# A two-layer decoder trunk on one core: rest parts and sums around the gating unit's two seams moved to VectorE and widened

## The chip, the cores and the metric

The kernel runs on one core of a Trainium2 chip. The core has TensorE (PE in the profile, with its weight loads as PEld), VectorE (DVE), ScalarE (ACT), GpSimd (POOL) and SyncE (SP), whose queue issues most of the DMAs. Each engine works through its own instructions in order and waits on the others by semaphores. The metric is the device time of one execution in microseconds (us), as the median of three runs. All stage times below are counted from the start of the profiled span.

## The reference

The program computes two layers on 1024 tokens of width 1024. Layer 0 is latent attention, layer 1 a chunked gating unit; the change touches the gating unit alone.

```python
def sgu_branch(xn, w_in, ln_g, ln_b, w_s, b_s):
    u, v, gate = jnp.split(xn @ w_in, 3, axis=-1)          # three parts of 2048
    u = jax.nn.gelu(u, approximate=False)
    v = layer_norm(jax.nn.gelu(v, approximate=False), ln_g, ln_b)
    vb = v.reshape(B, S // CHUNK, CHUNK, SGU_GROUPS, SGU_GW)   # chunks of 128, 16 groups of 128
    w = jnp.where(tri[None], w_s, 0).astype(v.dtype)           # lower triangle
    sv = jnp.einsum('gts,bcsgd->bctgd', w, vb) + b_s.T[None, None, :, :, None]
    return u * sv.reshape(B, S, BRANCH_W) * jax.nn.silu(gate)

# layer 1 of the trunk, then the end
x = x + sgu_branch(rms_norm(x, norm_g[1]), ...) @ sgu_w_o
return rms_norm(x, final_g)
```

## The kernel before

**Numbers in two parts.** Each fp32 operand of a product is split into a high part (rounded to the matmul's format, written by ScalarE, line 100) and a rest part (the operand less its high part, line 101, on VectorE or GpSimd). A product is then three matmuls: high by high, high by rest, rest by high. In the rows `wh` and `wl` are the two parts of a weight tile, and `x` on line 101 or 816 is a tile that holds both parts of an activation.

**The projection (`sgu`).** The product with `w_in` is cut into 12 groups: u0, gate0, u1, gate1, four of v, u2, gate2, u3, gate3. Each group is a 2 x 2 block product done with seven products instead of eight (steps 1, 5, 6, 7, 2, 4, 3). The weight sums of a step are made on VectorE (lines 775 to 788); `prep` then splits the tile. The activation has four quarters in each block: `b11`, `b21` are the two halves of the channels for the first 512 tokens, `b12`, `b22` those for the last 512 (a "half" below is 512 tokens). Its seven sums or differences are made in place, once, by `sums(i)`, and split into `X[i]`; all groups use them. The order of steps is a list, `steps`: (0, 1), (1, 1), (0, 2), (1, 2), then 5, 6, 7, 4, 3, each for group 0 and group 1, then group after group. The weight tiles of a step are prepared two steps ahead (`ahead`), in four buffers that go round.

**The first seam.** Layer 0 ends with eight out-projection tiles `po` (added to `x` on line 548), and layer 1 starts with steps 1 and 2 of groups 0 and 1, which need only the first half of the tokens. The half's RMS scale is made as sum of squares (line 155), `rstd` (line 148 on VectorE, the power on GpSimd, line 149) and `spread` (lines 176 to 187: diagonal matrices, two matmuls into a bank `rb`). `normed` (line 917) applies it. The second half's squares are summed on line 904, its scale follows after step (0, 2), and is spread between the two halves of step (1, 2). Only then can `sums(5)` start.

**The second seam.** During the last group, `second_stage` starts the mixing of channel pair p = 0: `shift` and eight calls of `unit`, each with matmuls into a bank `sv` (there are two such banks at that time), two VectorE instructions that read it (lines 1096 and 1099, tile `ht`), and at the end of each half the product with u times gate (line 1102) and the split of the result (lines 100 and 101). `load_out(p)` loads and splits two tiles of the output weights. Then come, for p = 0 to 6, the out-projection items of p merged with the mixing of p + 1. `norm(p)` scales and splits v (line 1061 on ScalarE) once its DMA is in.

The order of the instructions on each engine comes out of a scheduler that works on the program as it is written. The list therefore moves in places that the diff doesn't name.

Of the kernel before, what the change touches and what calls it, by code (L numbers as in the profile page):

```python
# [66 lines left out]
class Builder:  # L67
# [658 lines left out]
    def sgu(self):  # L726
# [5 lines left out]
        with ExitStack() as st:  # L732
# [16 lines left out]
            with ExitStack() as s2:  # L749
# [18 lines left out]
                def prep(g, i):  # L768
                    R = lambda n: RAW[g, n]
                    if i == 1:  # L770
                        z = R("a0")
                    elif i == 5:
                        z = R("b1") if g < 2 else rp.tile([P, 1024], F32, tag="raw", name=self.nm("sum"))
                        RAW[g, "s"] = z
                        v.tensor_tensor(z, R("b0"), R("b1"), op=ALU.add)
                    elif i == 6:
                        z = R("s")
                        v.tensor_tensor(z, z, R("a0"), op=ALU.subtract)
                    elif i == 7:
                        z = R("b0")  # L780
                        v.tensor_tensor(z, R("a0"), z, op=ALU.subtract)
                    elif i == 2:
                        z = R("a1")
                    elif i == 4:
                        z = R("b1")
                    else:
                        z = R("s")
                        v.tensor_tensor(z, R("a1"), z, op=ALU.subtract)
                    wh, wl = (self.wp.tile([P, 1024], F32R, tag=t, name=self.nm(t)) for t in ("wh", "wl"))
                    self.split(wh, wl, z, nc.gpsimd if i in (1, 2, 4) else v)  # L790
                    return wh, wl


# [158 lines left out]


                def sums(i):
                    for k in range(4):
                        b11, b21, b12, b22 = (q_(kh, t, k) for t in range(2) for kh in range(2))
                        if i == 5:
                            normed(1, k)
                            v.tensor_tensor(b11, b12, b11, op=ALU.subtract)
                            cut(5, k, b11)  # L960
                        elif i == 6:
                            normed(1, 4 + k)
                            v.tensor_tensor(b11, b22, b11, op=ALU.subtract)
                            cut(6, k, b11)
                        elif i == 7:
                            v.tensor_tensor(b12, b22, b12, op=ALU.subtract)
                            cut(7, k, b12)
                        elif i == 4:
                            v.tensor_tensor(b21, b21, b11, op=ALU.subtract)
                            cut(4, k, b21)  # L970
                        else:
                            cut(3, k, b22)

                for q, (g, i) in enumerate(steps):
                    if g == 0 and i in (5, 6, 4, 3):
# [10 lines left out]
                    if q == 0:  # L986
                        for z in range(2):
                            open_banks(z, 1, B)
                        for k in range(4):
                            for z in range(2):  # L990
                                for s in range(2):
                                    quarter_product(z, 1, W[z], B, s, 0, k)
                        ahead(3)
                        work = self.wp.tile([P, 1024], F32R, tag="wl", name=self.nm("work"))
                        work = [work[:, half(z)] for z in range(2)]
                    elif q > 1:
                        product(g, i, W[q], B, (lambda: share(1, work)) if q == 3 else None)
                    if q == 2:
                        b = ps.tile([P, HALF], F32, tag="x", name=self.nm("ssq"))[:, :4]
                        for f in later:  # L1000
                            f()
                        v.tensor_tensor(tot[1, 0], tot[1, 0], tot[1, 1], op=ALU.add)
                        self.token_sums(b, tot[1, 0])
                        self.rstd(r[:, 4:], b, 1.0 / D, EPS)
# [19 lines left out]
    def second_stage(self, rs, nmr, ln, operand, rp, ps, pse):  # L1024
# [41 lines left out]
        def mix(p):  # L1066
# [12 lines left out]
            def unit(h, j, e):  # L1079
# [19 lines left out]
                nc.vector.scalar_tensor_tensor(th, b[:, :, 0], gain, th, op0=ALU.mult, op1=ALU.add)  # L1099
                if e == 1:  # L1100
                    t = t.rearrange("p c t -> p (c t)")
                    nc.gpsimd.tensor_tensor(t, t, U[p, j][:, half(h)], op=ALU.mult)  # L1102
                    self.split(hh[:, half(h)], hl[:, half(h)], t, nc.gpsimd)
            return [(1, shift)] + [(2, lambda z=z: unit(*z)) for z in np.ndindex(2, 2, 2)]

        def load_out(p):
            out = []
            for j in range(2):
                f = rp.tile([P, D], F32, tag="raw", name=self.nm("wf"))
                nc.sync.dma_start(f, a["w_so"][2 * p + j])  # L1110
                h, l = (self.wp.tile([P, 1024], F32R, tag=z, name=self.nm(z)) for z in ("wh", "wl"))
                for c in range(2):
                    self.split(h[:, half(c)], l[:, half(c)], f[:, half(c)], nc.gpsimd)
                out.append((h, l))
            return out

# [229 lines left out]
```

## Time and profile before

| | us |
|---|---|
| three runs | 1703.13, 1704.98, 1706.16 |
| median | 1704.98 |
| the profiled execution, device time | 1708.3 |
| its span, first to last instruction | 1706.6 |
| TensorE busy | 1664.1 |
| VectorE busy | 1084.5 |
| ScalarE busy | 730.2 |
| GpSimd busy | 566.8 |

The profiled execution is 3.3 us longer than the median of the runs, and 1.7 us of its time lie outside its span. [...] The engines' busy times overlap, and that of TensorE is made of matmuls that follow each other every 0.227 us (512 columns at the upper level).

### The profile page before, as it was taken

How to read it: one execution, taken by the hardware profiler on the slowest of the kernel's cores; microseconds unless marked ns; L12 is line 12 of the kernel's file. 1: busy time of each engine (PE TensorE's matmuls, PEld its weight loads, DVE VectorE, ACT ScalarE, POOL GpSimd, SP SyncE). 2: the span in 40 equal slices, each digit the busy share in tenths (PEclk: the TensorE clock that was granted, in tenths of full speed). 3: DMA queues.
4: the chain of work that ended last, by engine and by line, in shares of the span. 5: the costliest groups of instructions: out<-in, count | busy, mean ns of one | idle time of the engine just before them, and what ended most of it. 6: DMA issues, size and time to landing. Idle time of an engine off the chain costs nothing. (4 is left out here: it accounts for less than half of the span.)

```text
span 1706.6 us, 23986 instructions
## 1 busy us (share of the span) xinstructions
PE 1664.1 (98%) x9150; PEld 1440.3 (84%) x9150; DVE 1084.5 (64%) x2008; ACT 730.2 (43%) x1301; POOL 566.8 (33%) x423
## 2 busy tenths in 40 slices
PE   8999999999999999999999988999999999899996
PEld 7888888888888888888888767889999888788886
DVE  7452111777777777777777699545555444688977
ACT  6233222644444444444444556433333335544225
POOL 5355561211212121121211323232112252676663
PEclk9999999999999999999999999999999999899998
DMA  5054542211111110111110423223232143634302
GB/s 191 13 156 150 159 161 86 62 33 32 53 32 53 32 53 32 53 33 52 35 54 19 136 93 106 74 93 112 101 114 102 50 156 129 223 116 149 105 26 99
DMA packets 66884, 150.50 MB, mean 88 GB/s; under 512 B 9296, under 2 KB 19024, under 8 KB 65744
## 3 DMA queue, kind: packets, MB, share of 16 engines
q1 hardware_dynamic: 57152, 125.89, 22.8%
q10 hardware_dynamic: 9616, 23.07, 3.6%
q8 instruction: 72, 1.18, 0.3%
q14 instruction: 44, 0.36, 0.1%
HBM read 106.07 MB, written 38.15 MB: 85 GB/s over the span
## 5 line engine op out<-in xcount | busy, mean ns | idle before, releaser
L101 POOL TENSOR_TENSOR wl<-wf,wh 128x512 fp32r<-128x512 f32 (+1 forms) x156 | 196.3, 1276 | 402.7 <-ACT wh L100 402.2
L101 POOL TENSOR_TENSOR wl<-raw,wh 128x1024 fp32r<-128x1024 f32 x36 | 87.9, 2443 | 246.9 <-ACT wh L100 217.9
L606 ACT ACTIVATE p<-s,mx 128x128 f32<-128x128 f32 (+7 forms) x128 | 95.0, 742 | 124.2 <-DVE mx L604 122.3
L100 ACT ACTIVATE th<-pt 128x512 fp32r<-128x512 f32 (+1 forms) x160 | 88.4, 552 | 139.3 <-PE pt L630 138.5
L100 ACT ACTIVATE wh<-wf 128x512 fp32r<-128x512 f32 (+2 forms) x158 | 87.2, 582 | 88.8 <-PE pj L122 50.4
L816 PE MATMUL px<-x,wh 128*128 128x512 f32 x384 | 118.7, 390 | 1.6 <-ACT x L100 1.5
L121 PE MATMUL pj<-xnh,wh 128*128 128x512 f32 x304 | 119.5, 393 | 0.0
L122 PE MATMUL pj<-xnl,wh 128*128 128x512 f32 x304 | 119.2, 392 | 0.0
L123 PE MATMUL pj<-xnh,wl 128*128 128x512 f32 x304 | 119.1, 392 | 0.0
L101 DVE TENSOR_TENSOR tl<-pt,th 128x512 fp32r<-128x512 f32 (+1 forms) x160 | 101.1, 632 | 27.1 <-ACT th L100 26.2
L121 PE MATMUL po<-x,wh 128*128 128x512 f32 (+1 forms) x288 | 109.9, 382 | 0.0
L548 DVE TENSOR_TENSOR xt<-xt,po 128x512 f32<-128x512 f32 x128 | 87.4, 683 | 32.4 <-PE po L123 31.8
L121 PE MATMUL po<-oh,wh 128*128 128x512 f32 x256 | 106.5, 416 | 0.0
L122 PE MATMUL po<-x,wh 128*128 128x512 f32 (+1 forms) x288 | 105.7, 367 | 0.6 <-POOL x L101 0.6
L123 PE MATMUL po<-x,wl 128*128 128x512 f32 (+1 forms) x288 | 106.1, 368 | 0.0
L123 PE MATMUL po<-oh,wl 128*128 128x512 f32 x256 | 101.4, 396 | 0.0
L122 PE MATMUL po<-ol,wh 128*128 128x512 f32 x256 | 100.9, 394 | 0.0
L603 DVE TENSOR_REDUCE mx<-s 128x1 f32<-128x128 f32 (+7 forms) x128 | 96.8, 757 | 3.0
L1127 DVE TENSOR_TENSOR xt<-xt,po 128x512 f32<-128x512 f32 (+1 forms) x144 | 86.3, 621 | 16.2 <-PE po L123 15.9
L421 DVE TENSOR_TENSOR gate<-pj,rb 128x512 f32<-128x512 f32 x32 | 22.0, 690 | 116.1 <-PE pj L123 115.5
L630 PE MATMUL pt<-ident,p 128*128 128x128 f32 x576 | 90.3, 273 | 0.5 <-DVE p L608 0.4
L816 PE MATMUL py<-x,wh 128*128 128x512 f32 x256 | 84.1, 408 | 6.4 <-DVE x L101 5.1
(273 smaller groups left out, 4848.7 us busy)
## 6 DMA issues: line engine op xcount, KB each, us to landing
raw<-w_u_dram SPq DMA_DIRECT2D x18, 512.0 KB, 3.6
raw<-w_sg_dram SPq DMA_DIRECT2D x18, 512.0 KB, 3.7
wf<-w_gate_dram SPq DMA_DIRECT2D x32, 256.0 KB, 3.3
gate<-gate ACTq DMA_DIRECT2D x16, 512.0 KB, 3.9
wf<-w_o_dram SPq DMA_DIRECT2D x32, 256.0 KB, 2.8
gate<-gate SPq DMA_DIRECT2D x32, 256.0 KB, 2.6
raw<-w_v_dram SPq DMA_DIRECT2D x16, 512.0 KB, 3.5
v<-xt ACTq DMA_DIRECT2D x32, 256.0 KB, 2.0
```

What stands on the lines that cost most here:

```text
L100: self.nc.scalar.activation(hi, src, AF.Copy)
L101: (eng or self.nc.vector).tensor_tensor(lo, src, hi.bitcast(F32), op=ALU.subtract)
L121: nc.tensor.matmul(out, lh, rh, start=first, stop=False)
L122: nc.tensor.matmul(out, lh, rl, start=False, stop=False)
L123: nc.tensor.matmul(out, ll, rh, start=False, stop=last)
L421: nc.vector.tensor_tensor(g[:, c], b, rb[:, c], op=ALU.mult)
L548: nc.vector.tensor_tensor(x, x, st[m], op=ALU.add)
L603: nc.vector.tensor_reduce(mx, b, axis=AX.X, op=ALU.max)
L606: nc.scalar.activation(pr, b, AF.Exp, bias=mx, scale=SCALE, accum_out=sm)
L630: nc.tensor.transpose(b[:, w:w + P], PR[n, 4 * h + i][:, k * P:(k + 1) * P], self.ident)
L816: nc.tensor.matmul(o, l_, m_, start=opens and n == k == e == 0, stop=closes and n == 2 and k == 3 and e == (kind == "v"), skip_group_check ...
L1127: nc.vector.tensor_tensor(x, x, b, op=ALU.add)
```

## The change

Five edits, all in the gating unit:

1. The rest parts of the weight tiles of steps 1, 2 and 4 of groups 0 and 1 (six instructions of 128 x 1024) are made on VectorE instead of GpSimd.
2. `sums` works on several quarters at once: step 6 on two at a time, steps 7, 4 and 3 on all four, step 5 still on one. The difference and both parts of the split are one instruction each for 1024 or 2048 columns instead of 512.
3. The sums of the second half's squares and its scale are written after step (0, 1) instead of (0, 2), the spread inside step (0, 2) instead of (1, 2).
4. In `unit`, for p = 0, the product with u times gate and its rest part are on VectorE (four of each).
5. In `load_out`, for p = 0, the four rest parts are on VectorE.

```diff
-                    self.split(wh, wl, z, nc.gpsimd if i in (1, 2, 4) else v)
+                    self.split(wh, wl, z, nc.gpsimd if i in (1, 2, 4) and g > 1 else v)
...
                 def sums(i):
-                    for k in range(4):
-                        b11, b21, b12, b22 = (q_(kh, t, k) for t in range(2) for kh in range(2))
-                        if i == 5:
-                            normed(1, k)
-                            v.tensor_tensor(b11, b12, b11, op=ALU.subtract)
-                            cut(5, k, b11)
...
+                    n = {5: 1, 6: 2}.get(i, 4)
+                    for k in range(0, 4, n):
+                        b11, b21, b12, b22 = (
+                            self.xt[:, 4 * kh + k:4 * kh + k + n, half(t)] for t in range(2) for kh in range(2)
+                        )
+                        if i in (5, 6):
+                            for z in range(n):
+                                normed(1, (4 if i == 6 else 0) + k + z)
+                        a, b, out = {5: (b12, b11, b11), 6: (b22, b11, b11), 7: (b22, b12, b12),
+                                     4: (b21, b11, b21), 3: (b22, None, b22)}[i]
+                        if b is not None:
+                            v.tensor_tensor(out, a, b, op=ALU.subtract)
+                        self.split(X[i][:, 0, k:k + n], X[i][:, 1, k:k + n], out)
...
-                        product(g, i, W[q], B, (lambda: share(1, work)) if q == 3 else None)
-                    if q == 2:
+                        product(g, i, W[q], B, (lambda: share(1, work)) if q == 2 else None)
+                    if q == 0:
...
                 if e == 1:
-                    nc.gpsimd.tensor_tensor(t, t, U[p, j][:, half(h)], op=ALU.mult)
-                    self.split(hh[:, half(h)], hl[:, half(h)], t, nc.gpsimd)
+                    e = nc.gpsimd if p else nc.vector
+                    e.tensor_tensor(t, t, U[p, j][:, half(h)], op=ALU.mult)
+                    self.split(hh[:, half(h)], hl[:, half(h)], t, e)
...
-                    self.split(h[:, half(c)], l[:, half(c)], f[:, half(c)], nc.gpsimd)
+                    self.split(h[:, half(c)], l[:, half(c)], f[:, half(c)], nc.gpsimd if p else nc.vector)
```

What that does to VectorE's order at three places. The first is the start of the first seam, from the first half's sum of squares (`ssq`) to the first sums of step 1. Before:

```order
L735 CAST ones_r<-ones 128x128
L148 TENSOR_SCALAR small<-ssq_9966 128x4
L548 TENSOR_TENSOR xt<-xt,po_9989 128x512
L176 CAST rsh_9975<-small 128x4
L177 TENSOR_TENSOR rsl_9976<-small,rsh_9975 128x4
L186 TENSOR_SCALAR work_9973<-ident,rsh_9975 128x128 x4
L548 TENSOR_TENSOR xt<-xt,po_9999 128x512
L904 TENSOR_TENSOR x_2000_9915<-x_2000_9915 128x512
L548 TENSOR_TENSOR xt<-xt,po_10009 128x512
L917 SCALAR_TENSOR_TENSOR xt<-xt,ng,rb_9944 128x512 x3
```

And now:

```order
L735 CAST ones_r<-ones 128x128
L101 TENSOR_TENSOR wl_9929<-raw_9916,wh_9928 128x1024
L148 TENSOR_SCALAR small<-ssq_9966 128x4
L548 TENSOR_TENSOR xt<-xt,po_9989 128x512
L176 CAST rsh_9975<-small 128x4
L548 TENSOR_TENSOR xt<-xt,po_9999 128x512
L177 TENSOR_TENSOR rsl_9976<-small,rsh_9975 128x4
L186 TENSOR_SCALAR work_9973<-ident,rsh_9975 128x128 x4
L548 TENSOR_TENSOR xt<-xt,po_10009 128x512
L101 TENSOR_TENSOR wl_9933<-raw_9920,wh_9932 128x1024
L917 SCALAR_TENSOR_TENSOR xt<-xt,ng,rb_9944 128x512 x3
```

One weight rest part stands ahead of line 148, a second ahead of the first line 917; GpSimd has only the power of line 149 left here.

The second place is steps 6 and 7 of the activation, from the last scaling with `rb` on. `x_1996` is X[6], `x_1997` X[7]. Before:

```order
L917 SCALAR_TENSOR_TENSOR xt<-xt,ng,rb_9945 128x512 x2
L101 TENSOR_TENSOR x_1996_9911<-xt,x_1996_9911 128x512 x2
L963 TENSOR_TENSOR xt<-xt 128x512 x2
L101 TENSOR_TENSOR wl_10374<-raw_9924,wh_10373 128x1024
L101 TENSOR_TENSOR x_1996_9911<-xt,x_1996_9911 128x512 x2
L966 TENSOR_TENSOR xt<-xt 128x512 x2
L863 TENSOR_TENSOR cx<-px_10344,cx 128x512
L101 TENSOR_TENSOR x_1997_9912<-xt,x_1997_9912 128x512
```

And now:

```order
L917 SCALAR_TENSOR_TENSOR xt<-xt,ng,rb_9945 128x512 x2
L101 TENSOR_TENSOR x_1996_9911<-xt,x_1996_9911 128x1024
L966 TENSOR_TENSOR xt<-xt 128x2x512
L101 TENSOR_TENSOR wl_10368<-raw_9924,wh_10367 128x1024
L966 TENSOR_TENSOR xt<-xt 128x4x512
L101 TENSOR_TENSOR x_1996_9911<-xt,x_1996_9911 128x1024
L966 TENSOR_TENSOR xt<-xt 128x4x512
L863 TENSOR_TENSOR cx<-px_10338,cx 128x512
L863 TENSOR_TENSOR cx<-px_10339,cx 128x512
L101 TENSOR_TENSOR x_1997_9912<-xt,x_1997_9912 128x2048
```

The differences of steps 7 and 4 (128x4x512) now stand around the second rest part of step 6, and the rest part of step 7 comes as a whole after both reads of `px` (line 863).

The third place is the mixing of pair p = 0 in the second seam, around the banks `sv`; `x_2342` and `x_2320` with 128x1024 are splits of v for later pairs. Before:

```order
L1099 SCALAR_TENSOR_TENSOR ht_13819<-sv_13844,lngb,ht_13819 128x256
L871 TENSOR_TENSOR cx<-px_13689,cx 128x512
L101 TENSOR_TENSOR x_2320_13673<-x_2315_13641,x_2320_13673 128x1024
L871 TENSOR_TENSOR cx<-px_13690,cx 128x512
L1096 SCALAR_TENSOR_TENSOR ht_13819<-sv_13888,lngb,bs 128x256
L101 TENSOR_TENSOR x_2342_13887<-x_2315_13641,x_2342_13887 128x1024
L1099 SCALAR_TENSOR_TENSOR ht_13819<-sv_13888,lngb,ht_13819 128x256
```

And now (lines 1091 and 1094 are the former 1096 and 1099, line 1098 the former 1102; `x_2335` is the rest part of `ht`):

```order
L1094 SCALAR_TENSOR_TENSOR ht_13789<-sv_13814,lngb,ht_13789 128x256
L871 TENSOR_TENSOR cx<-px_13660,cx 128x512
L1098 TENSOR_TENSOR ht_13789<-ht_13789,x_2325_13691 128x512
L1091 SCALAR_TENSOR_TENSOR ht_13789<-sv_13858,lngb,bs 128x256
L1091 SCALAR_TENSOR_TENSOR ht_13789<-sv_13865,lngb,bs 128x256
L1094 SCALAR_TENSOR_TENSOR ht_13789<-sv_13858,lngb,ht_13789 128x256
L101 TENSOR_TENSOR x_2335_13782<-ht_13789,x_2328_13735 128x512
L1094 SCALAR_TENSOR_TENSOR ht_13789<-sv_13865,lngb,ht_13789 128x256
```

Between the two reads of the fifth bank (`sv_13888` before, `sv_13858` now) there stood a split of v; there now stands the first read of the sixth bank. Both splits of `x_2342` come after the eighth bank, those of `x_2320` after the first additions of the out-projection.

## Rows read from the trace of the kernel before

**Rows 1.** By stretch: busy us (count) of PE, PEld, DVE, ACT, POOL; clock; DMA.
```profile
970.00:1080.00 110.00, 97.38 (x404) 76.96 (x404) 97.96 (x132) 63.65 (x90) 33.04 (x17) 0.95 0.36 119
1080.00:1465.00 385.00, 385.00 (x2341) 346.31 (x2339) 193.88 (x261) 149.56 (x202) 113.05 (x62) 1.00 0.31 108
1465.00:1485.00 20.00, 14.19 (x56) 11.63 (x56) 13.84 (x18) 9.91 (x17) 16.11 (x11) 0.74 0.58 184
1485.00:1650.00 165.00, 165.00 (x823) 138.39 (x823) 137.75 (x251) 60.39 (x105) 109.70 (x83) 1.00 0.33 120
```
**Rows 2.** Waits of TensorE, 970 to 1080: total us, times, longest.
```profile
PE py L816 <- DVE x L101: 5.1, 3, 2.3
PE pb L816 <- DVE xt L548: 2.3, 2, 1.7
PE rb L187 <- DVE work L186: 1.9, 1, 1.9
PE px L816 <- ACT x L100: 1.5, 1, 1.5
PE py L816 <- ACT x L100: 1.3, 1, 1.3
```
**Rows 3.** Waits of TensorE, 1465 to 1485.
```profile
PE sv L1093 <- DVE ht L1099: 5.8, 1, 5.8
```
**Rows 4.** TensorE by stretch: busy (matmuls), granted clock, DMA share, GB/s.
```profile
977.00:981.00 4.00, 4.00 (x11) 0.59 0.98 355
1015.00:1019.00 4.00, 3.80 (x10) 0.57 0.01 2
1067.00:1070.00 3.00, 3.00 (x8) 0.52 0.22 87
1470.00:1479.50 9.50, 6.41 (x19) 0.50 0.73 227
```
**Rows 5.** Groups by form, 970 to 1080: busy us, mean ns, idle before.
```profile
L101 DVE TENSOR_TENSOR x<-xt,x 128x512 fp32r<-128x512 f32 x28 | 25.3, 939 | 0.3 <-ACT x L100 0.3
...
L101 POOL TENSOR_TENSOR wl<-raw,wh 128x1024 fp32r<-128x1024 f32 x7 | 18.4, 2627 | 40.9 <-PE px L816 26.4 <-ACT wh L100 11.9 <-ACT x L100 2.5
...
L966 DVE TENSOR_TENSOR xt<-xt 128x512 f32<-128x512 f32 x4 | 2.6, 685 | 0.0
...
L101 DVE TENSOR_TENSOR wl<-sum,wh 128x1024 fp32r<-128x1024 f32 x2 | 2.4, 1224 | 0.7 <-issue 0.7
```
**Rows 6.** Timeline of GpSimd from 972: start, duration, instruction, idle before.
```profile
972.30 2.40 POOL L101 TENSOR_TENSOR wl<-raw,wh 128x1024 fp32r<-128x1024 f32 x1 [1.99 <-ACT wh L100]
...
984.34 5.22 POOL L101 TENSOR_TENSOR wl<-raw,wh 128x1024 fp32r<-128x1024 f32 x2 [4.02 <-ACT wh L100]
```
**Rows 7.** Timeline of VectorE in the first seam.
```profile
986.37 3.73 DVE L101 TENSOR_TENSOR x<-xt,x 128x512 fp32r<-128x512 f32 x2
...
1008.63 1.41 DVE L917 SCALAR_TENSOR_TENSOR xt<-xt,ng,rb 128x512 f32<-128x512 f32 x2 [1.21 <-PE rb L187]
...
1062.28 5.04 DVE L101 TENSOR_TENSOR x<-xt,x 128x512 fp32r<-128x512 f32 x3
```
**Rows 8.** Timeline of GpSimd in the second seam.
```profile
1465.98 2.25 POOL L1102 TENSOR_TENSOR ht<-ht,x 128x512 f32<-128x512 f32 x1
```
**Rows 9.** Timeline of ScalarE in the second seam and behind it.
```profile
1468.27 0.63 ACT L100 ACTIVATE x<-ht 128x512 fp32r<-128x512 f32 x1 [2.17 <-POOL ht L1102]
...
1494.30 1.59 ACT L1061 ACTIVATE x<-x,small 128x256 f32<-128x256 f32 x3 [6.84 <-DMA x<-v]
```
**Rows 10.** Timeline of VectorE in the second seam.
```profile
1470.39 2.15 DVE L101 TENSOR_TENSOR x<-x,x 128x1024 fp32r<-128x1024 f32 x1 [2.30 <-ACT x L100]
1472.47 0.47 DVE L1099 SCALAR_TENSOR_TENSOR ht<-sv,lngb,ht 128x256 f32<-128x256 f32 x1
```
**Rows 11.** Timeline of GpSimd where the out-projection of pair 1 starts.
```profile
1506.22 1.29 POOL L101 TENSOR_TENSOR x<-ht,x 128x512 fp32r<-128x512 f32 x1 [0.74 <-ACT x L100]
```
**Rows 12.** Timeline of TensorE at the same place.
```profile
1507.87 0.39 PE L122 MATMUL po<-x,wh 128*128 128x512 f32 x1
```

More of the change, by code (lines that the diff above doesn't have):

```diff
@@ L954, in sums @@
                 def sums(i):
-                    for k in range(4):
-                        b11, b21, b12, b22 = (q_(kh, t, k) for t in range(2) for kh in range(2))
-                        if i == 5:
-                            normed(1, k)
-                            v.tensor_tensor(b11, b12, b11, op=ALU.subtract)
-                            cut(5, k, b11)
[L961 to L972, printed above, removed]
+                    n = {5: 1, 6: 2}.get(i, 4)
[11 more added lines that the diff above has]
+                        self.split(X[i][:, 0, k:k + n], X[i][:, 1, k:k + n], out)
                 for q, (g, i) in enumerate(steps):
```

## The prediction

> **What bounds the kernel now.** I read the busy times by stretch first [rows 1]. TensorE has no idle time from 1080 to 1465 and from 1485 to 1650, at the upper clock: there only fewer matmuls would save time, and the change leaves their number as it is. It loses time at two seams. From 970 to 1080 it is busy 97.4 of 110 us at a mean clock of 0.95, and VectorE is busy 98.0 of the 110. From 1465 to 1485 it is busy 14.2 of 20 us at 0.74.
>
> The waits of TensorE say for whom. In the first seam they add up to 12.1 us, nearly all for VectorE, or for a ScalarE split that itself follows VectorE [rows 2]. In the second it is one wait of 5.8 us for the second read of an `sv` bank [rows 3].
>
> A wait costs more than its length. Behind the waits the granted clock falls to about 0.5 [rows 4]. At 0.227 us per matmul the 11 matmuls from 977 to 981 need 2.5 us and take 4.0: 1.5 lost. From 1015 the 10 matmuls take 3.8 instead of 2.3 us: again 1.5. From 1067 the 8 take 3.0 instead of 1.8: 1.2. In the second seam 6.4 busy us at half clock lose 3.2. So the first seam costs 12.1 + 4.2 = 16.3 us, the second 5.8 + 3.2 = 9.0. These 25 us are all there is to win.
>
> **First seam, the moved rest parts.** Six GpSimd splits of 2.63 us become VectorE splits of 1.22 [rows 5], 7.3 us more for an engine that is already 89% busy there. Two things pay for them. GpSimd's split at 972.30 takes 2.40 us and stands ahead of the power in the first scale [rows 6]. Now the scale waits only for a 1.22 us split on VectorE. I put the bank `rb` about 1 us earlier and, as its two matmuls also stand later in TensorE's order, the 1.9 us wait at 0.6; a wait of 0.6 needs no clock loss behind it. Worth 1.3 + 1.5 = 2.8.
>
> Second, a VectorE instruction whose two inputs lie in SBUF stands still while GpSimd runs one: two splits from 986.37 took 3.73 us, ending 0.5 us after GpSimd's pair (984.34 + 5.22 = 989.56) [rows 6, 7], where 2 x 0.685 would do. The 28 splits of 512 columns average 0.939 against 0.685 [rows 5], 7.1 us in all; about 5 of these I trace to the six moved splits. So VectorE's added work is 7.3 - 5 = 2.3 us, less about 1 for the wide forms. The 2.3 us that TensorE waited for line 548 become about 1.6: that line now follows the scaling by 4 us instead of 6, but TensorE arrives almost 3 us sooner. Worth 0.7, and 3.5 up to the end of step 1.
>
> Wide forms: 1224 - 685 = 539 ns for 512 further columns [rows 5], so 128x2048 is estimated at 2.3 us, on ScalarE at about 2.0. Back to back, two of 512 took 1.28 to 1.41 on VectorE's timeline against 1.22 for one of 1024, a gain of some 0.1 us each. [...]
>
> **First seam, the second scale.** Its chain starts after the seven additions of squares, which now stand in a row. I follow VectorE's new order with these durations: the first scaling with the second `rb` comes at about 1006.7 instead of 1008.63 [rows 7]. TensorE, 3.5 us ahead, still waits for it, longer than now (about 4 us, with the clock loss), and ends step 5 only 1.5 us ahead. Bounds: 0 if the four remaining GpSimd products of line 853 hold VectorE there for another 1.5 us, 3.5 if the scale keeps pace.
>
> Step 6: its rest parts are now ready two at a time, 1 to 3 us ahead of the matmuls that read them, so the 1.5 us wait [rows 2] goes: 3.0 ahead. Step 7: TensorE gets nothing until all 2048 columns are split, behind both reads of `px`. By my walk that is some 0.4 us late: 2.6 ahead. Bounds: 0 to 3 (ScalarE 2.0 + VectorE 2.3 against 0.63 + 0.69 for a quarter). Steps 4 and 3: three quarter splits took 5.04 us from 1062.28 [rows 7] between two GpSimd instructions, and TensorE waited 3.0 us (two of the three waits behind 5.1) and lost 1.2 at half clock. Now the whole rest part stands earlier, at about 1054 to 1056, before TensorE needs it at 1058. Both come back: 2.6 + 4.2 = 6.8. I take **6.5** for the seam, with 3 and 8.5 as its bounds.
>
> **Second seam.** The 5.8 us wait goes back in a line: the second read of `sv` stood behind a split of v (1470.39, 2.15 us) [rows 10]; that waited for ScalarE, which had waited 2.17 us for GpSimd's product (1465.98, 2.25 us) [rows 8, 9]. GpSimd came to it late because it had four weight splits, and the products of line 853 between them. Now GpSimd has neither weights nor `ht`. VectorE takes over twelve instructions of 0.69 us, 8.2 us, in a stretch where it idles a third of the time, and the split of v stands behind the eighth bank. What is late next is VectorE: its reads come up to 1 us after TensorE wants the bank, four times, so I leave 1 us of the 9.0. Worth 8.
>
> Not all of it arrives. The out-projection of pair 1 needs its own rest parts, and GpSimd ended the second of them at 1506.22 + 1.29 = 1507.5 [rows 11], 0.36 us before the matmul that reads it, at 1507.87 [rows 12]. That chain starts with ScalarE, which waited 6.84 us for a DMA of v, until 1494.30 [rows 9]. The DMA queue holds this load until an earlier v is split and x is fetched. By the new order it is issued about 3.5 us sooner, not 8, and behind it GpSimd's queue is as long as before. I put the rest part at 1501.5, 6 us sooner, so 2 of the 8 are given back as a new wait at pair 1. Worth **6**, with bounds 3.5 (a clock loss there as well, and the DMA no more than 5 us sooner) and 8. Later pairs have over 2 us in hand and run as now.
>
> Sum: 6.5 + 6 = 12.5. The profiled 1708.3 become 1695.8; its 3.3 us over the median taken off, **1692.5 us**.
>
> **Rivals.** (A) The first seam wins nothing: VectorE sets its pace, and 2.3 us more work with whole-row splits makes new waits at steps 5 and 7 (2 + 3 us and 1.5 of clock) in place of 6.5 us won. For it: 98 of 110 us busy. Against it: a tenth of those are waits for GpSimd that go. Then 1704.98 - 6 = 1699. (B) The second seam gives its 8 us back at pair 1 but for 1 us, since the DMA of v is bound by the volume of x, u, v and weights that goes through at once; 1704.98 - 7.5 = 1697.5. (C) The other sign: the hold itself. VectorE issues six wide and twelve short two-input instructions more, and the products left on GpSimd hold them. If all 7.1 us of holding stay in the first seam, the added 7.3 us fall on the path with one more clock loss of 1.5, 8.8 us lost; if eight products of 1.29 us in the second seam also hold VectorE, 10 us, its 9.0 are lost again and 1 more. Then 1704.98 + 9.8 = 1714.8. It decides once VectorE is held for more than some 6 us that are free now. Against it: far fewer GpSimd instructions remain. [...] (D) The waits only move, and both scale and v bind as now: within 0.2%, 1704.
>
> **How the numbers follow.** Forecast 0.64, A 0.12, B 0.10, C 0.06, D 0.08. The forecast's own range, from 9 to 16 us won, is 1689 to 1696. With A and B, and some width for a second clock loss, the range is **1686.5 to 1700.5**; it leaves out C and D and the edges. No change means within 0.2%, 3.4 us, about what three runs can tell: faster 0.86, the same 0.08, slower 0.06.
>
> **What would show it.** Line 101 on GpSimd from 970 to about 1070 once instead of seven times; 18 GpSimd instructions fewer in all. No wait of TensorE for line 548 over 1.7 us, none of 2 us at step 3, but one of 3 to 5 us at step 5. No half clock around 978 and 1068. In the second seam no wait over 1.5 us for the second `sv` read, and the first out-projection about 8 us nearer to the last projection step. At pair 1 a wait of about 2 us, for GpSimd. The step most likely wrong is the walk through step 5 and 7: an order says what follows what, not when, and a slip of 1 us decides whether the clock falls.

## The result and the profile after

Four runs of the changed kernel gave 1693.23 to 1696.28 us, median 1695.13; four of the kernel before, on the same chip, 1703.13 to 1706.16, median 1704.22. The ratio is 0.9935 with a 95% interval of 0.9922 to 0.9949, that is 11 us (9 to 13) faster; the two medians alone are 9.1 us apart. The predicted 12.5 us lie inside the interval, near its upper end. The forecast time of 1692.5 us is 2.6 us below the measured median, which lies inside the forecast's range. Measured once more on another chip (run 9 below) the ratio was 0.9928 (0.9909 to 0.9947). The sum came near; both seams' terms were off, in opposite directions.

The profiled execution took 1695.74 us (span 1693.9, mean clock 0.992). Its stretches, with the columns of [rows 1], the third one new:

```profile
970.00:1080.00 110.00, 102.97 (x444) 83.00 (x444) 98.92 (x120) 63.35 (x80) 24.16 (x13) 0.98 0.35 120
1465.00:1485.00 20.00, 20.00 (x103) 16.86 (x102) 15.75 (x29) 9.18 (x17) 5.73 (x6) 1.00 0.68 245
1485.00:1540.00 55.00, 51.36 (x239) 42.23 (x238) 45.47 (x79) 24.19 (x45) 40.06 (x30) 0.94 0.34 125
```

TensorE's idle time in the first stretch fell from 12.6 to 7.0 us, the second stretch is full, and a hole has opened in the third, where TensorE had none before. GpSimd did 17 instructions in the first stretch and does 13. The waits of TensorE from 970 to 1080, against [rows 2]:

```profile
PE py L816 <- ACT x L100: 4.2, 1, 4.2
PE pb L816 <- DVE xt L548: 1.3, 1, 1.3
PE rb L187 <- DVE work L186: 1.0, 1, 1.0
PE px L816 <- DVE x L101: 0.3, 1, 0.3
PE py L816 <- DVE x L101: 0.2, 1, 0.2
```

One long wait is left, the one at step 5. The groups by form, against [rows 5]:

```profile
L101 POOL TENSOR_TENSOR wl<-raw,wh 128x1024 fp32r<-128x1024 f32 x3 | 7.9, 2636 | 8.3 <-ACT c L852 4.2 <-ACT wh L100 4.1
L101 DVE TENSOR_TENSOR x<-xt,x 128x512 fp32r<-128x512 f32 x12 | 7.9, 684 | 0.0
...
L101 DVE TENSOR_TENSOR x<-xt,x 128x2048 fp32r<-128x2048 f32 x3 | 7.4, 2454 | 0.0
...
L966 DVE TENSOR_TENSOR xt<-xt 128x2048 f32<-128x2048 f32 x2 | 4.6, 2287 | 0.0
```

GpSimd has three weight splits instead of seven in this stretch (the first at 1054.62), and a VectorE split of 512 columns takes 0.684 us instead of 0.939: nothing holds it any more. The wide splits still average 2.454 us, where a difference of the same 2048 columns takes 2.287.

**A ledger.** The times at which TensorE starts the same matmul show where the time came from. The first matmul on the squares' sums stands ahead of everything that the change touches, and came at 970.37 before and 967.47 now: 2.9 us are not the change's. The other columns are "ahead of before" in us, worked out from such times, with each kernel's difference at that first mark taken off. A number that grows from one row to the next is time won in between, one that falls is time given back.

| TensorE starts | before | changed | ahead: changed | changed, again | first seam alone | second seam alone | pair 1's weights too |
|---|---|---|---|---|---|---|---|
| sums of squares | 970.37 | 967.47 | 0 | 0 | 0 | 0 | 0 |
| step 1 | 984.69 | 978.84 | 2.95 | 3.05 | 3.03 | 1.69 | 3.03 |
| step 5 | 1011.94 | 1007.93 | 1.11 | 1.24 | 1.17 | 2.04 | 1.17 |
| step 6 | 1028.59 | 1021.03 | 4.66 | 5.05 | 5.00 | 1.17 | 4.87 |
| step 3 | 1061.73 | 1054.32 | 4.51 | 4.92 | 4.90 | 1.13 | 4.76 |
| group 2 | 1077.66 | 1065.20 | 9.56 | 9.97 | 9.95 | 1.02 | 9.81 |
| first out-projection | 1480.97 | 1460.17 | 17.90 | 18.38 | 10.42 | 9.41 | 18.20 |
| weight sums of pair 2 | 1508.33 | 1492.34 | 13.09 | 14.14 | 9.47 | 7.23 | 18.21 |
| weight sums of pair 3 | 1534.46 | 1520.73 | 10.83 | 11.77 | 9.43 | 7.21 | 17.27 |
| last sums of squares | 1695.54 | 1682.79 | 9.85 | 10.88 | 8.64 | 6.50 | 17.29 |

The first seam won 9.56 us where 6.5 were predicted. The second won 17.90 - 9.56 = 8.3 (predicted 8), and by pair 3 17.90 - 10.83 = 7.1 of them were given back (predicted 2).

**Two columns that were not the change's.** The second-seam column is of a kernel whose first seam is as before, and it is "1.02 ahead" there; two more such kernels are 1.79 and 1.88 ahead. The clock tells why. TensorE from 40 to 60 and from 975 to 985, before and then in one of these kernels, that of run 10 (the granted clock is the third number from the end of a line; in stretches of 0.5 us of before it is 1.00, the upper level, or 0.50, half clock, or a figure between in a stretch in which it changes, and at 0.50 matmuls of 512 columns start 0.43 us apart):

```profile
40.00:60.00 20.00, 20.00 (x92) 17.07 (x91) 8.47 (x24) 5.19 (x13) 3.50 (x3) 0.83 0.09 16
975.00:985.00 10.00, 7.46 (x25) 5.69 (x26) 7.93 (x17) 7.04 (x12) 4.05 (x3) 0.83 0.82 283
```

```profile
40.00:60.00 20.00, 20.00 (x106) 17.13 (x105) 8.46 (x25) 5.78 (x14) 3.50 (x3) 1.00 0.08 15
975.00:985.00 10.00, 8.77 (x38) 6.66 (x36) 10.00 (x14) 6.29 (x10) 5.73 (x3) 1.00 0.76 281
```

The profiled execution of before fell to half clock (0.50 from 978.0 to 981.0) behind a 1.9 us wait; there run 10 waited 1.3 us and kept its clock. About 1.6 us (the mean of 1.02, 1.79 and 1.88) of the first seam's 9.56 belong to that one execution. What the change wins there is about 8.0. The length of the wait alone doesn't decide it: run 12 waited as long for the same matmul and kept the upper level.

```profile
973.90 0.50 PE L187 MATMUL rb<-work,ones_r 128*128 128x512 f32 x1 [1.93 <-DVE work L186]
```

```profile
975.00:985.00 10.00, 7.62 (x31) 5.16 (x30) 9.68 (x14) 6.21 (x11) 2.37 (x1) 1.00 0.54 207
```

The stretch from 40 to 60, far ahead of the change, shows 0.83, 0.91 or 1.00 in nine profiles (before, the changed kernel, which has 0.91 twice, and runs 1 to 3 and 10 to 12), and with it the first mark lies at 970 to 971, 967 to 969 or 966 to 967. The scatter between profiles has that as one source.

### The profile page after: what moved, and what is told of

The parts are those of the page before. It is cut to its first block, busy times and chain, and to the rows that moved or that the text cites. A ratio compares the mean times of both kernels' runs of the same rounds, so it can differ in the third digit from the quotient of the medians.

```text
span 1693.9 us, 23943 instructions
## 1 busy us (share of the span) xinstructions
PE 1659.1 (98%) x9150; PEld 1437.1 (85%) x9150; DVE 1094.9 (65%) x2007; ACT 728.6 (43%) x1290; POOL 531.9 (31%) x405
## 4 chain that ended last, share of the span: by engine, by line
PE 92%; DVE 3%; POOL 2%; ACT 2%; issue 1%; DMA 0%; POOLq 0%; SPq 0%; ACTq 0%; DVEq 0%
PE px L816 11%; PE py L816 8%; PE pb L816 8%; PE pj L121 7%; PE pj L122 7%; PE pj L123 7%; PE po L121 6%; PE po L123 6%; PE po L122 6%; PE pt L630 4%; PE pv L123 3%; PE pv L121 3%; PE pv L122 3%; PE s L121 2%; PE s L122 2%; PE s L594 2%
## 5 line engine op out<-in xcount | busy, mean ns | idle before, releaser
L101 POOL TENSOR_TENSOR wl<-wf,wh 128x512 fp32r<-128x512 f32 (+1 forms) x152 | 189.0, 1261 | 404.1 <-ACT wh L100 403.5
L101 POOL TENSOR_TENSOR wl<-raw,wh 128x1024 fp32r<-128x1024 f32 x30 | 72.7, 2424 | 209.7 <-ACT wh L100 202.5
L121 PE MATMUL po<-x,wh 128*128 128x512 f32 (+1 forms) x288 | 111.4, 387 | 2.3 <-ACT x L100 1.6
L122 PE MATMUL po<-x,wh 128*128 128x512 f32 (+1 forms) x288 | 107.6, 374 | 2.2 <-POOL x L101 2.2
L1123 DVE TENSOR_TENSOR xt<-xt,po 128x512 f32<-128x512 f32 (+1 forms) x144 | 86.6, 621 | 15.7 <-PE po L123 15.2
L100 ACT ACTIVATE wh<-raw 128x1024 fp32r<-128x1024 f32 x54 | 56.8, 1056 | 67.1 <-PE py L816 24.8
```

Source lines behind the costliest of these rows:

```text
L100: self.nc.scalar.activation(hi, src, AF.Copy)
L101: (eng or self.nc.vector).tensor_tensor(lo, src, hi.bitcast(F32), op=ALU.subtract)
L121: nc.tensor.matmul(out, lh, rh, start=first, stop=False)
L122: nc.tensor.matmul(out, lh, rl, start=False, stop=False)
L1123: nc.vector.tensor_tensor(x, x, b, op=ALU.add)
```

## The experiments

Twelve experiments, each against runs of the kernel before on the same chip. A gain in us is worked out from the ratio; the difference of the medians lies up to 2 us from it. "Ahead" is by the ledger.

**1. The first seam alone** (edits 1 to 3). The diff is against the changed kernel: it takes edits 4 and 5 back.

```diff
-                    e = nc.gpsimd if p else nc.vector
-                    e.tensor_tensor(t, t, U[p, j][:, half(h)], op=ALU.mult)
-                    self.split(hh[:, half(h)], hl[:, half(h)], t, e)
+                    nc.gpsimd.tensor_tensor(t, t, U[p, j][:, half(h)], op=ALU.mult)
+                    self.split(hh[:, half(h)], hl[:, half(h)], t, nc.gpsimd)
...
-                    self.split(h[:, half(c)], l[:, half(c)], f[:, half(c)], nc.gpsimd if p else nc.vector)
+                    self.split(h[:, half(c)], l[:, half(c)], f[:, half(c)], nc.gpsimd)
```

> Kernel before plus the three edits of the first seam (rest parts, wide sums, sooner scale); the second seam as before. Theory (the seams add up, and the first seam won about 9.6 us between the squares' sums and the seventh step's end in the profiles): 9 to 10 us faster than before, so about as fast as the whole change; TensorE's 5.8 us wait for the second sv bank is there again, and no wait at the start of the next pair's out-projection. Rival (the first seam gives the 6.5 us predicted, and the rest of its 9.6 us is spread between two executions): 6 to 7 us faster.

Ratio 0.9950 (0.9935 to 0.9965), 8.5 us faster (6 to 11). Ahead by 9.95 at group 2 and 8.64 at the end; the 5.9 us wait for `sv` is there. Together with the 1.6 us above this lies between the two expectations: about 8.4 won, part of the 9.6 from one execution.

**2. The second seam alone** (edits 4 and 5 on the kernel before).

```diff
-                    nc.gpsimd.tensor_tensor(t, t, U[p, j][:, half(h)], op=ALU.mult)
-                    self.split(hh[:, half(h)], hl[:, half(h)], t, nc.gpsimd)
+                    e = nc.gpsimd if p else nc.vector
+                    e.tensor_tensor(t, t, U[p, j][:, half(h)], op=ALU.mult)
+                    self.split(hh[:, half(h)], hl[:, half(h)], t, e)
...
-                    self.split(h[:, half(c)], l[:, half(c)], f[:, half(c)], nc.gpsimd)
+                    self.split(h[:, half(c)], l[:, half(c)], f[:, half(c)], nc.gpsimd if p else nc.vector)
```

> Kernel before plus the two edits of the second seam alone (product and rest parts of pair 0, and its four weight splits, on VectorE). Theory (won 8.3 us at the last projection step, 7.1 us given back one pair later): within 0.5 to 2 us of before, faster; the 5.8 us wait gone, waits of 3 to 4 us and half a clock when pair 1's out-projection starts. Rival (the give-back belongs to the two seams together): 5 to 6 us faster, as predicted for this seam.

Ratio 0.9965 (0.9953 to 0.9977), 6.0 us faster (4 to 8). The theory fell: alone, this seam keeps what the prediction gave it. It won 9.41 - 1.02 = 8.4 and gave back 2.2. The same instructions in the same order give back 2.2 here and 7.1 in the changed kernel. ScalarE here, and TensorE (two stretches of 4 us) where pair 1's out-projection starts:

```profile
1484.89 5.04 ACT L1061 ACTIVATE x<-x,small 128x256 f32<-128x256 f32 x10 [9.75 <-DMA x<-v]
1489.83 0.62 ACT L100 ACTIVATE x<-ht 128x512 fp32r<-128x512 f32 x1
```

```profile
1495.38:1499.38 4.00, 3.31 (x16) 2.25 (x15) 3.96 (x7) 1.52 (x3) 4.00 (x4) 1.00 0.00 0
1499.38:1503.38 4.00, 3.02 (x15) 2.60 (x16) 3.02 (x7) 3.37 (x7) 3.26 (x3) 1.00 0.19 47
```

And in the changed kernel: ScalarE, GpSimd, and TensorE in stretches of 4 us:

```profile
1474.80 4.05 ACT L1056 ACTIVATE x<-x,small 128x256 f32<-128x256 f32 x8 [10.82 <-DMA x<-v]
1479.88 1.09 ACT L1056 ACTIVATE x<-x,small 128x256 f32<-128x256 f32 x2 [1.03 <-DMA x<-v]
1480.87 0.61 ACT L100 ACTIVATE x<-ht 128x512 fp32r<-128x512 f32 x1
...
1488.84 0.63 ACT L100 ACTIVATE x<-ht 128x512 fp32r<-128x512 f32 x1 [3.83 <-POOL ht L1098]
```

```profile
1476.81 1.30 POOL L1098 TENSOR_TENSOR ht<-ht,x 128x512 f32<-128x512 f32 x1 [1.29 <-DVE ht L1094]
1481.57 1.30 POOL L101 TENSOR_TENSOR x<-ht,x 128x512 fp32r<-128x512 f32 x1 [3.45 <-ACT x L100]
1482.82 4.76 POOL L101 TENSOR_TENSOR wl<-wf,wh 128x512 fp32r<-128x512 f32 x3
1487.53 1.27 POOL L1098 TENSOR_TENSOR ht<-ht,x 128x512 f32<-128x512 f32 x1
1488.76 1.28 POOL L101 TENSOR_TENSOR wl<-wf,wh 128x512 fp32r<-128x512 f32 x1
1490.00 1.27 POOL L101 TENSOR_TENSOR x<-ht,x 128x512 fp32r<-128x512 f32 x1
```

```profile
1484.17:1488.17 4.00, 3.02 (x15) 2.13 (x14) 3.09 (x5) 0.84 (x1) 4.00 (x3) 1.00 0.00 0
1488.17:1492.17 4.00, 1.35 (x3) 0.94 (x4) 2.20 (x5) 3.09 (x6) 4.00 (x4) 0.77 0.00 0
1492.17:1496.17 4.00, 4.00 (x13) 3.23 (x12) 3.62 (x6) 1.89 (x3) 3.26 (x3) 0.50 0.48 164
1496.17:1500.17 4.00, 4.00 (x19) 3.31 (x19) 4.00 (x10) 0.63 (x1) 1.89 (x2) 0.87 0.59 205
```

ScalarE's order has ten scalings of v (eight of pair 3, two of pair 4) ahead of pair 1's first high part. Here pair 4's v was in when its turn came, and the ten stand in a row: the two loads landed 7.1 and 4.8 us after their issue. In the changed kernel, which issues them as far behind the first out-projection matmul as here (6.3 and 11.6 us), they took 8.3 and 8.1 us from their issue to the scaling that they let go (1466.51 to 1474.80, 1471.76 to 1479.88). ScalarE stopped twice, and the first high part came 20.70 us after the first out-projection matmul instead of 18.45. TensorE then lost 3.6 us to waits instead of 1.7, the clock fell to half behind them, and that cost the other 3.4 (7.1 - 3.6).

**3. The changed kernel with pair 1's four weight splits on VectorE too.**

```diff
-                    self.split(h[:, half(c)], l[:, half(c)], f[:, half(c)], nc.gpsimd if p else nc.vector)
+                    self.split(h[:, half(c)], l[:, half(c)], f[:, half(c)], nc.gpsimd if p > 1 else nc.vector)
```

> The changed kernel, with the four weight splits of pair 1 on VectorE as well. Theory Q (GpSimd's queue: the weight splits stand between the first and the second rest part of pair 1, 6 of the 9.7 us from 1481.57 to 1491.27): the waits of 1.6 and 1.3 us and the half clock behind them go, 4 to 6 us faster than the changed kernel, about 1690. Theory D (ScalarE is late because it stands waiting for the DMA of v, until 1474.80 and again until 1479.88, and everything behind it is late by as much): at most 1 us faster.

Median 1691.12, ratio 0.9911 (0.9896 to 0.9925), 15 us faster than before. As theory Q has it, nothing is given back at pair 1 (18.20, 18.21), and the end is 17.29 ahead, where the changed kernel was 9.85 and 10.88. GpSimd at the same place:

```profile
1481.94 1.29 POOL L101 TENSOR_TENSOR x<-ht,x 128x512 fp32r<-128x512 f32 x1 [1.48 <-ACT x L100]
1485.85 1.29 POOL L1098 TENSOR_TENSOR ht<-ht,x 128x512 f32<-128x512 f32 x1 [2.62 <-DVE ht L1094]
1487.88 1.29 POOL L101 TENSOR_TENSOR x<-ht,x 128x512 fp32r<-128x512 f32 x1 [0.74 <-ACT x L100]
```

GpSimd now idles 2.62 us ahead of the second product, which waits for VectorE. The v was early in this profile too (first high part 18.70 us after the first out-projection matmul), but by this slack a v that lands 2 us later should not have delayed that product, so that a late v would cost time only through the weight splits that queue behind the first rest part. That is argued: the three kernels without these splits on GpSimd (runs 3, 4 and 12) all have an early v in their profiles (first high part after 18.70, 18.49 and 17.97 us). What the queue costs behind an early v is 2.2 to 2.9 us (runs 2 and 8); how the rest of the changed kernel's 7 is shared between the queue and a late v, no profile separates.

**4. The same, with the norm of pair 2's v written behind pair 1's units.**

```diff
-                norm(p + 2, fetch(p + 2))
+                c = fetch(p + 2)
+                if p:
+                    norm(p + 2, c)
                 run(self.merge(items[head:], mix(p + 1)))
+                if p == 0:
+                    norm(p + 2, c)
```

> As the run with pair 1's weight splits on VectorE, and the norm of pair 2's v written behind pair 1's units instead of ahead of them, so that ScalarE comes to pair 1's high parts one activation sooner and TensorE to its sv banks one out-projection tile sooner. Theory Q: the same as without it within 1 us. Theory D: 1 to 3 us faster than without it.

Median 1690.03, ratio 0.9906 (0.9891 to 0.9922): the same within 1.1 us, as Q has it. ScalarE's order on the way to the first high part is one scaling shorter, no more, so this is a weak test of D. These two have the lowest medians of the study. Against the changed kernel their intervals touch its own; the ledger has run 3 ahead of it by 6.4 to 7.4 us.

**5. The moved rest parts alone** (edit 1).

```diff
-                    self.split(wh, wl, z, nc.gpsimd if i in (1, 2, 4) else v)
+                    self.split(wh, wl, z, nc.gpsimd if i in (1, 2, 4) and g > 1 else v)
```

> Kernel before plus the moved rest parts alone (six GpSimd splits of two groups to VectorE). By the prediction's walk: 3.5 us ahead up to the end of the second step, then part of it lost where the second scale is still late: 1 to 4 us faster than before. Rival (VectorE is the pace there, and 7.3 us more work costs more than the hold that goes): 1 to 4 us slower.

Ratio 1.0003 (0.9993 to 1.0012): no gain, and no loss. Both expectations missed. The splits of 512 columns fall to 0.835 us. But the 4.2 us wait at step 5 is there as in the changed kernel (0.77 ahead, where unchanged seams are about 2.0), and quarter splits are still waited for at step 3 (two waits, 2.6 us).

**6. The wide sums alone** (edit 2, the part of the change's diff on `sums`).

```diff
-                    for k in range(4):
...
+                    n = {5: 1, 6: 2}.get(i, 4)
+                    for k in range(0, 4, n):
...
+                        self.split(X[i][:, 0, k:k + n], X[i][:, 1, k:k + n], out)
```

> Kernel before plus the wide sums alone. By the prediction: they only save some 1 us of VectorE, and hide the waits of steps 6 to 3 by standing earlier as a whole: 1 to 5 us faster. Rival (a whole row must be split before TensorE gets anything): up to 3 us slower, with a new wait at the start of steps 6 or 7.

Ratio 0.9987 (0.9978 to 0.9996), 2.2 us faster, at the low end of the expected. Ahead 4.01 at group 2, 2.4 above the 1.6 of an unchanged seam.

**7. The sooner second scale alone** (edit 3).

```diff
-                        product(g, i, W[q], B, (lambda: share(1, work)) if q == 3 else None)
-                    if q == 2:
+                        product(g, i, W[q], B, (lambda: share(1, work)) if q == 2 else None)
+                    if q == 0:
```

> Kernel before plus the sooner second scale alone. By the prediction: the wait of step 5 shrinks by 1 to 2 us when VectorE is still held by GpSimd's splits: 0 to 3 us faster. Rival (the additions of squares now stand ahead of the scaling that TensorE waits for in the second step): up to 2 us slower.

Ratio 0.9977 (0.9966 to 0.9987), 3.9 us faster, a little over the expected. Step 6 starts 5.21 ahead, but TensorE then waits 3.1 us for ScalarE and 3.1 for VectorE in steps 6 to 4, and gets back only at step 3 (4.56 at group 2).

**8. The changed kernel without the wide sums.**

```diff
-                    n = {5: 1, 6: 2}.get(i, 4)
-                    for k in range(0, 4, n):
...
+                    for k in range(4):
...
```

> The changed kernel with the old quarter-wide sums (the other four edits kept). If the three edits of the first seam add up, slower than the changed kernel by what the wide sums alone win over before. Rival (with GpSimd's splits gone there is nothing to hold the short sums, so the wide form wins nothing more): within 1 us of the changed kernel.

Ratio 0.9957 (0.9942 to 0.9972), 7.3 us faster than before, some 4 less than the changed kernel. The rival fell, and the theory's sum was too small as well (the wide sums alone won 2.2). At group 2 it is 2.97 ahead instead of 9.56: the wide sums are worth 6.6 us there once the other two edits stand, and 2.4 by themselves. TensorE's waits are those that the prediction spoke of, quarter splits at step 3:

```profile
1059.34 0.50 PE L816 MATMUL py<-x,wh 128*128 128x512 f32 x1 [0.89 <-DVE x L101]
1062.11 0.72 PE L816 MATMUL py<-x,wh 128*128 128x512 f32 x1 [1.81 <-DVE x L101]
```

Pair 1 took back only 11.24 - 8.39 = 2.9 here; its first high part came 19.11 us after the first out-projection matmul.

**9. The changed kernel again**, with no edit.

> The changed kernel once more, with a profile of its own. In its first profile v landed 8.3 and 8.1 us after its issue, TensorE waited 3.6 us where pair 1's out-projection starts, ran at half clock behind it, and 7.1 us of the 8.3 won at the second seam were given back; the run with the second seam alone had v after 7.2 us, waits of 1.7 us, no half clock, and gave back 2.2. Theory J (the schedule is the same, and about 1 us in the landing of v decides whether the clock falls): the executions scatter by 4 us or more, the profile shows a give-back anywhere from 2 to 7 us that follows the landing of v, and the ratio is about 0.992 to 0.995. Theory F (with the first seam won too, the give-back is always 7): a give-back of 6 to 8 us whatever v does, and 9 us faster than before.

Ratio 0.9928 (0.9909 to 0.9947), six runs from 1690.43 to 1697.87. The first high part came 20.10 us after the first out-projection matmul, and 6.6 us were given back. With the numbers above that makes 18.45, 19.11, 20.10 and 20.70 us beside 2.2, 2.9, 6.6 and 7.1 us given back: theory J fits, with a step between 19.1 and 20.1. A first seam that is won doesn't by itself make v late: runs 3, 4 and 12 won it too, issue the first of the two loads at the same distance, and have their first high part after 17.97 to 18.70 us. J isn't settled against F, since both profiles of this very kernel lie above the step, and the kernel before scatters as widely (1700.72 to 1708.87).

**10. and 11. The second seam's two edits one at a time** on the kernel before: first the product and rest part (edit 4), then the weight splits (edit 5).

```diff
-                    nc.gpsimd.tensor_tensor(t, t, U[p, j][:, half(h)], op=ALU.mult)
-                    self.split(hh[:, half(h)], hl[:, half(h)], t, nc.gpsimd)
+                    e = nc.gpsimd if p else nc.vector
+                    e.tensor_tensor(t, t, U[p, j][:, half(h)], op=ALU.mult)
+                    self.split(hh[:, half(h)], hl[:, half(h)], t, e)
```

```diff
-                    self.split(h[:, half(c)], l[:, half(c)], f[:, half(c)], nc.gpsimd)
+                    self.split(h[:, half(c)], l[:, half(c)], f[:, half(c)], nc.gpsimd if p else nc.vector)
```

> Kernel before plus one edit of the second seam: product and rest part of pair 0 on VectorE, its four weight splits left on GpSimd. By the prediction, the wait came from GpSimd's product standing behind the weight splits: without the product the 5.8 us wait goes, 4 to 7 us faster than before. Rival (the weight splits themselves, then late, hold VectorE's new two-input instructions and the out-projection's start): 0 to 3 us faster, and a wait of 1 us or more at the first out-projection.

> Kernel before plus the other edit of the second seam: pair 0's four weight splits on VectorE, product and rest part left on GpSimd. GpSimd comes to its products about 5 us sooner, but each rest part still goes from VectorE to GpSimd to ScalarE to GpSimd. Theory (the queue on GpSimd made the wait): the 5.8 us wait shrinks to 0 to 2 us, 4 to 6 us faster. Rival (the chain from engine to engine made it): it stays at 4 us or more, 0 to 2 us faster.

The product alone: ratio 0.9973 (0.9962 to 0.9984), 4.6 us faster; 7.07 - 1.79 = 5.3 won at the first out-projection, a wait of 1.9 us for `sv` left, 1.6 given back. The weights alone: ratio 0.9995 (0.9983 to 1.0007), no change that shows. Yet they took the 5.8 us wait away but for 1.0 us (9.71 - 1.88 = 7.8 won at the first out-projection, so the queue on GpSimd made the wait), and by pair 3 9.71 - 1.56 = 8.2 us were given back: at pair 1 TensorE waited 1.7 us for ScalarE and 1.6 for a bank `sv`, and its clock fell to half (0.50 from 1504 to 1508). The theory was right on the wait, the rival on the time.

**12. The run of 3 with group 1's rest parts back on GpSimd.**

```diff
-                    self.split(wh, wl, z, nc.gpsimd if i in (1, 2, 4) and g > 1 else v)
+                    self.split(wh, wl, z, nc.gpsimd if i in (1, 2, 4) and g > 0 else v)
```

> The changed kernel with pair 1's weight splits on VectorE as well, and the rest parts of the second group of the first seam back on GpSimd (only the first group's moved). In the profile of the changed kernel VectorE has two splits of 1.2 and 1.5 us and a sum between the second rb and the sums that step 5 waits 4.2 us for, while GpSimd idles. Theory (VectorE's own work makes that wait): it shrinks to 2 to 3 us, 1 to 3 us faster than the run with pair 1's weight splits alone. Rival (each GpSimd split holds a pair of VectorE splits again): the same, or up to 3 us slower than that run.

Ratio 0.9929 (0.9910 to 0.9948), not faster than run 3. At step 5 the 4.2 us fell to 2.5, as the theory has it, but new waits stand elsewhere (970 to 1080), and the seam is 7.70 ahead instead of 9.81:

```profile
PE pb L816 <- DVE x L101: 2.4, 3, 1.9
PE px L816 <- ACT x L100: 1.9, 1, 1.9
PE rb L187 <- DVE work L186: 1.9, 1, 1.9
PE py L816 <- DVE x L101: 1.3, 1, 1.3
PE py L816 <- ACT x L100: 1.2, 1, 1.2
```

VectorE's splits of 512 columns are back at 0.822 us. TensorE kept the upper level through the whole stretch, so no clock loss is among them:

```profile
970.00:1080.00 110.00, 100.86 (x436) 79.90 (x435) 99.38 (x113) 62.66 (x80) 31.91 (x16) 1.00 0.33 117
```

The rival is the nearer one: the ledger's end is 15.2 ahead instead of 17.29, and the ratios lie some 3 us apart (0.9929 against 0.9911, on another chip, with intervals that overlap).

## Why the prediction was right, and where not

**First seam, the moved rest parts (predicted 3.5 up to the end of step 1).** Right in mechanism: 2.95 at the start of step 1, and behind it the second wait for line 548 (1.68 us) is gone, 4.6 in all. Kernels with this seam unchanged are 1.6 to 1.7 ahead at the same mark and wait 1.3 us behind it, so 2.1 of the 4.6 belong to before's execution and 2.5 to the change. Alone the edit wins nothing (run 5): the microseconds won here are waited away at steps 5 and 3 unless the other edits stand.

**The second scale (predicted 1.5 ahead at the end of step 5).** The wait of 3 to 5 us at step 5 came (4.2), with a half clock behind it (0.50 from 1009.5 to 1012.0). But TensorE was 4.66 ahead at the start of step 6, where 3.0 were predicted. Before, it had lost 3.3 us to two waits and 1.5 to the clock there; the second of these waits is gone (0.2). This term was too small by 1.7 us.

**Steps 6, 7, 4 and 3.** Step 7 cost 0.15 between the starts of steps 6 and 3 (predicted 0.4; a wait of 0.31 shows it). Step 3 brought 9.56 - 4.51 = 5.05 (predicted 4.2). Run 8 shows the reason as it was given: without the wide form the quarter splits wait there again. For the price of the wide form the durations are 0.680, 1.222 and 2.287 us for 512, 1024 and 2048 columns, so four of 512 one by one are 2.72. Back to back they cost less: six additions of 512 took 3.70 us, 0.617 each, so four are 2.47 against 2.29 for the wide one, as the sum had it. The prediction took about 1 us off for the wide forms, at some 0.1 an instruction; on VectorE 19 instructions go (28 splits became 17, and 16 differences 8), which at 0.1 each is nearer 2 us, and 1.1 at the 0.06 of these additions. Run 8 has the same seam lose 6.6 us without them: wide instructions won more by where they stand than by what they save.

**The seam's sum.** 6.5 was predicted with 3 and 8.5 as bounds; the profiles show 9.6 to 10.0, outside. The 3.1 us between 6.5 and 9.56 are the second scale (1.7), step 3 (0.9), step 7 (0.2) and the rounding of 6.8 to 6.5 (0.3). Another step failed beside these sizes: the 1.5 us of half clock around 978 were booked as the kernel's, and only the execution profiled before shows them. Without that execution's 1.6 us the seam won 8.0 to 8.4, inside the bounds, near the upper one.

**Second seam.** The 8 won were 8.3, and by the mechanism named: run 11 takes 4.8 of the 5.8 us of wait away by emptying GpSimd's queue, run 10 takes 3.9.

**Given back at pair 1 (predicted 2, bounds 0 and 4.5).** 7.1 and 6.6 in the two profiles of the changed kernel, 2.2 with the second seam alone. The place, ScalarE's stop for v and the queue on GpSimd were named; the size failed. By the prediction the second rest part would end 6 us sooner. Less the 12.46 us by which all of this stretch had moved (9.56 and the 2.9 of the first mark), its chain gained this: the load of v that ScalarE waits for was issued 15.14 - 12.46 = 2.7 us sooner (1486.90 to 1471.76; predicted 3.5), it landed 2.0 sooner, the first rest part started 2.5 sooner, and the second ended (1507.51 to 1491.27) 3.8 sooner. And no clock loss was in the 2; behind 3.6 us of waits it was 3.4. Rival B is what the profile shows (1.3 us of the second seam are left), but the volume of the loads, its reason, isn't what run 3 shows: with the same loads, and a v that was early, nothing is given back there.

**The rest.** GpSimd has 18 instructions fewer. Rivals A, C and D fell: the seam won, and VectorE's short splits were no longer held (0.684 us). That GpSimd can be held instead shows as well: three splits took 4.76 us beside a VectorE split at 1485.04, and 3.81 in run 2. VectorE's own hold shows before on the two splits from 986.37 [rows 7], and not on line 548 ahead of them, which reads TensorE's `po` and took 0.68 us at 985.77 beside the same pair on GpSimd. The hold on GpSimd doesn't explain what is given back: run 8 has it as well (4.83 us) and gave back 2.9, and in run 2 the product behind the three splits took 2.31 us instead of 1.27, so GpSimd lost 1 us there too.

The forecast held because two errors went against each other: the first seam gave 1.5 us more than its term (3 by the profiles as they are), the second 4 to 5 less. What is left is somewhat below 12.5: the ledger ends 9.85 and 10.88 ahead, 1.6 of it by before's execution, and the medians are 9.1 and 10.8 us apart. That the total came so near is in part luck.

## What to carry to other kernels

When a stall is taken away, follow the next consumer of every queue that the stall was covering: here most of the second seam's win was lost some 27 us later, behind weight splits on GpSimd that TensorE had not waited for before, and with four more moved instructions (run 3) it was kept. Price a wait with the half clock that may follow it, and look for that clock in more than one execution before it is booked as a gain. Edits that win nothing alone can be the condition for another's gain (the rest parts 0, the wide sums 2 alone, and 6.6 at the seam on top of the others), so test them by leaving out as well as by adding.

## What was not expected of the hardware

- The same instructions, far from the change, ran at a mean clock of 0.83, 0.91 or 1.00 from 40 to 60 us, and what follows moved with it, by up to 5 us (first mark from 966.24 to 971.27).
- A load of v (1 MB) took from 4.9 to 8.2 us to land in one profile; in four profiles of the same order of instructions the first high part behind it moved by 2.3 us, and the time given back went in a step from 2.9 to 6.6.
- Where pair 1 starts, waits of 1.7 and 2.3 us in all left TensorE at the upper level (runs 2 and 8), and waits of 3.1 and 3.6 us (run 9 and the changed kernel) were followed by the lower one for some 7 us (0.50 from 1490.5 to 1497.0 in the changed kernel), at a price of 3.4 us there. In the first seam a single wait of 1.9 us was followed by it in before's execution and not in run 12 (0.83 and 1.00 from 975 to 985).
